# Down projections: the gate and the addition of x1 spread one step per entry, and x1 for the norm loaded one tile per entry

## The chip, the cores and the metric

The kernel runs as one program on one core of a Trainium2 chip. The metric is the device time of one execution in microseconds (us). The kernel before took 2372.89 us, the median of three runs from 2371.21 to 2376.52. The profile shows one further execution of it.

## The reference, cut to what matters

One decoder layer over 2048 rows of width 1024. Attention and short convolution come first, then the ConvFFN, in whose last lines everything around this change lies:

```python
    x = x + g1 * (mixed @ w_out)                          # called x1 below

    h2 = rmsnorm(x, norm2_g) * (1 + sc2) + sh2
    u = causal_dwconv(h2 @ w_up, ffn_conv_w)
    u_gate, u_val = jnp.split(u, 2, axis=-1)
    y = (jax.nn.silu(u_gate) * u_val) @ w_down            # D_FF = 2816 to 1024
    return x + g2 * y
```

All tensors are float32. What is computed at the end is therefore, for each block of the output, a sum of matrix products, times the gate g2, plus x1.

## The kernel before, in words

**Stages.** The rows are worked in two halves of 1024 rows. The stages follow each other on TensorE: mixing (attention, convolution, output projection), then up(0), down(0), up(1), down(1), where up computes `h2 @ w_up` with convolution and silu for one half, and down the product with `w_down`. The norm of the second half (row blocks Q = 2 and 3 of 512 rows each) is not done ahead: its work, `norm2_late(2)` and `norm2_late(3)`, runs inside down(0) as side work. x1 lies in DRAM by then (`x1_sc`, one tensor for each 128 rows).

**A down projection.** It is one level of Strassen-Winograd multiplication: seven products p = 0 to 6 (the table `plan`) yield four output blocks of 512 rows by 512 columns. Each product sums over j = 0 to 10 (D_FF / 256 = 11 steps). `todo` lists the 77 pairs (p, j), here called entries. Four PSUM tiles `acc[t]`, t = 0 to 3, hold 128 rows each of the sum. An entry's operands come as one raw tile of two halves (y and w, 256 KB each), which ScalarE and VectorE split into a high part `hi` (L1528) and a low part `lo` = raw - hi (L1529). Each acc tile of an entry then takes three matmuls, hi by hi, hi by lo, lo by hi, so an entry is 12 matmuls of 128x128 by 128x512 (L1762). The entry j = 9 issues none, and j = 10 does those of 9 and 10 together, tile by tile, so that tile t is complete 6 matmuls after tile t - 1.

**Order within an entry.** `K` keeps instructions in the order in which the program issues them, on each engine. An entry issues in this order: the split (hi, lo) of the operands of the entry two ahead, the loads of raw tiles five ahead (SyncE's queue, SP; four raw buffers), stores that were put off (`flush`), the loads of x1 for an output block (`x1_tiles`, at the entries that `extra` names), the matmuls, at j = 10 the evictions `evict(p, t)`, and one step of the side work (`next(side)`). VectorE and ScalarE therefore see evictions and side work in one line with the splits that the coming entries need.

**Evictions.** Products 0 to 2 and 3 to 6 build sums in `u2` and `u3`. A block is finished in product 1 (block (0, 0): row half 0, column half 0), 4 (block (0, 1)), 5 (block (1, 1)) and 6 (block (1, 0)). Finishing is `finish_block`: multiply by the gate (L1715), add x1 (`xs`, through `add`, L1440), store to `out` (L1717). In products 4, 5 and 6 an addition with u2 or u3 stands ahead of it. All of it is issued for a tile at once, at that tile's eviction. Products 0, 2, 3 and 5 begin in fresh PSUM tiles (`banks`); products 1, 4 and 6 add on to the tiles of the product before them, so that the first matmul of product 6 on tile t waits for product 5's eviction of that tile.

**Side work in down(0).** A step of `norm2_late` is taken per entry. In order: the last three steps of up's last pair (they store y and its differences), then for Q = 2 the loads of x1 (L1353, four transfers of 512 KB in one step), three empty steps, four steps with one squaring each on ScalarE (L1358), the row factors, the scaling (L1365), and then transposes, `hi`/`lo` pairs and sums (L1260, L1267, L1408). For Q = 3 the same follows, with more sums per step on VectorE.

Of the kernel before, what the change touches and what calls it, by code (L numbers as in the profile page):

```python
# [9 lines left out]
F32 = mybir.dt.float32  # L10
F32R = mybir.dt.float32r
F16 = mybir.dt.float16
BF16 = mybir.dt.bfloat16
I32 = mybir.dt.int32
AF = mybir.ActivationFunctionType
# [5 lines left out]
P = 128  # L21
S = 2048
D = 1024
# [19 lines left out]
NTEMP = 7  # L43
# [3 lines left out]
def kernel(  # L47
# [19 lines left out]
    nc = tc.nc  # L67
    V, A, G, T = nc.vector, nc.scalar, nc.gpsimd, nc.tensor
    x, c, out = x[0], c[0:1], out[0]
# [71 lines left out]
    K = tc.keep_in_program_order  # L141
# [1101 lines left out]
    with ExitStack() as ph:  # L1243
# [25 lines left out]
        xn = {}  # L1269
# [78 lines left out]
        def norm2_late(Q):  # L1348

            ss = fp.tile([P, 16], F32, tag="ss", name="ss", bufs=2)[:, 0:4]  # L1350
            xn[Q] = [wide_temp()[:, 0:D] for _ in range(4)]
            for t in range(4):
                K(nc.sync.dma_start(xn[Q][t], x1_sc[Q * 4 + t]))  # L1353
            for _ in range(3):
                yield
            for t in range(4):
                junk = fp.tile([P, D], BF16, tag="t2", name="junk", bufs=NTEMP)
                K(A.activation(junk, xn[Q][t], AF.Square, accum_out=ss[:, t : t + 1]))  # L1358
                yield
            K(V.tensor_scalar(ss, ss, 1.0 / D, EPS, op0=ALU.mult, op1=ALU.add))  # L1360
            for ins in rsqrt_steps(fp, ss, 4, "r"):
                K(ins)
            yield
            for t in range(4):
                K(V.tensor_scalar(xn[Q][t], xn[Q][t], ss[:, t : t + 1], None, op0=ALU.mult))  # L1365
                if t % 2:
                    yield
            later = []
            if Q % 2 == 0:
                for k in range(4):  # L1370
                    for n, name in enumerate(("b11", "b21")):
                        affine = turn(Q, 4 * n + k)
                        if later:
                            later.pop()()
                        yield
                        h = affine()
                        hi, lo = pair(name, k)
                        high(h, hi)
                        later.append(lambda h=h, hi=hi, lo=lo: low(h, hi, lo))
                        yield  # L1380
                later.pop()()
                yield
                return

            def sums(k, b1, b2):

                b22, t1s, t2s, t3s, t4s = [pair(name, k) for name in ("b22", "t1", "t2", "t3", "t4")]
                b11, b21 = bt["b11", k], bt["b21", k]
                t3 = temp()
                high(b2, b22[0])  # L1390
                diff(t3, b2, b1)
                diff(b1, b1, b11[0])
                diff(b1, b1, b11[1])
                low(b2, *b22)
                yield
                high(b1, t1s[0])
                high(t3, t3s[0])
                yield
                diff(b2, b2, b1)
                low(b1, *t1s)  # L1400
                low(t3, *t3s)
                yield
                high(b2, t2s[0])
                yield
                t4 = temp()
                diff(t4, b21[1], b2)
                low(b2, *t2s)
                K(V.tensor_tensor(t4, t4, b21[0], op=ALU.add))  # L1408
                yield
                high(t4, t4s[0])  # L1410
                yield
                low(t4, *t4s)
                yield

            running = []

            def go_on():
                for g in list(running):
                    if next(g, 1):
                        running.remove(g)  # L1420

            for k in range(4):
                first = turn(Q, k)
                go_on()
                yield
                b1 = first()
                go_on()
                yield
                second = turn(Q, 4 + k)
                go_on()  # L1430
                yield
                b2 = second()
                go_on()
                running.append(sums(k, b1, b2))
                yield
            while running:
                go_on()
                yield
# [251 lines left out]
        def down(hv, side):  # L1690

            todo = [(p, j) for p in range(7) for j in range(NJ)]
            loaded = split = 3
            rows = [[slice((Q * 4 + t) * P, (Q * 4 + t + 1) * P) for t in range(4)] for Q in (2 * hv, 2 * hv + 1)]
            u2, u3 = [[fb.tile([P, 512], F32, tag=f"src{4 * n + t}", name="u") for t in range(4)] for n in range(2)]
            gate = [gates[:, D + n * 512 : D + (n + 1) * 512] for n in range(2)]
            xs = {}

            def x1_tiles(c, n):
                xs[c, n] = [fb.tile([P, 512], F32, tag=f"wo{4 * c + t}1", name="xs") for t in range(4)]  # L1700
                for xp, r in zip(xs[c, n], rows[c]):
                    K(nc.sync.dma_start(xp, x1_sc[r.start // P][:, n * 512 : (n + 1) * 512]))

            def banks(kinds):
                return [
                    ps_d.tile([P, 512], F32, tag="d", name="acc") if k == "d" else ps_u.tile([P, 512], F32, tag="u", name="acc")
                    for k in kinds
                ]

            def rest():  # L1710
                return fp.tile([P, 1024], F32, tag="first", name="g", bufs=2)[:, 0:512]

            def finish_block(c, n, t, total):
                g = rest()
                K(V.tensor_tensor(g, total, gate[n], op=ALU.mult))  # L1715
                add(xs[c, n][t], xs[c, n][t], g)
                K(nc.sync.dma_start(out[rows[c][t], n * 512 : (n + 1) * 512], xs[c, n][t]))  # L1717

            def evict(p, t):
                a = acc[t]  # L1720
                if p == 0:
                    K(A.activation(u2[t], a, AF.Copy))
                elif p == 1:
                    finish_block(0, 0, t, a)
                elif p == 2:
                    add(u2[t], u2[t], a)
                elif p == 3:
                    add(u3[t], u2[t], a)
                elif p == 5:
                    add(u3[t], u3[t], a)  # L1730
                    finish_block(1, 1, t, u3[t])
                else:
                    g = rest()
                    add(g, u2[t], a)
                    finish_block(*((0, 1) if p == 4 else (1, 0)), t, g)

            extra = {(1, 2): (0, 0), (4, 2): (0, 1), (5, 2): (1, 1), (6, 3): (1, 0)}
            for e, (p, j) in enumerate(todo):
                while split < min(e + 3, len(todo)):
                    if loaded == split:  # L1740
                        raws[todo[loaded]] = load_operands(hv, *todo[loaded])
                        loaded += 1
                    pairs[todo[split]] = split_pair(raws.pop(todo[split]))
                    split += 1
                while loaded < min(e + 6, len(todo)):
                    raws[todo[loaded]] = load_operands(hv, *todo[loaded])
                    loaded += 1
                if (p, j) in ((0, 0), (0, 4)):
                    flush()
                if (p, j) in extra:  # L1750
                    x1_tiles(*extra[p, j])
                if j == 0 and p in (0, 2, 3, 5):
                    acc = banks({0: "dddd", 2: "uuud", 3: "dddu", 5: "uudd"}[p])
                if j != NJ - 2:
                    for t in range(4):
                        c = slice(t * P, (t + 1) * P)
                        for jj in (j,) if j < NJ - 1 else (j - 1, j):
                            yh, yl, wh, wl = pairs[p, jj]
                            for a, b, st, sp in (
                                (yh, wh, jj == 0 and p in (0, 2, 3, 5), False), (yh, wl, False, False), (yl, wh, False, jj == NJ - 1)  # L1760
                            ):
                                K(T.matmul(acc[t], lhsT=a[:, c], rhs=b, start=st, stop=sp, skip_group_check=True))  # L1762
                        if j == NJ - 1:
                            evict(p, t)
                next(side, None)
            for _ in side:
                pass
# [39 lines left out]
```

## Time and profile before

| | |
|---|---|
| median of three runs | 2372.89 us (2371.21 to 2376.52) |
| the profiled execution | 2373.66 us, span 2372.0 us, mean granted TensorE clock 0.994 |
| busy share of the span | PE 96%, VectorE (DVE) 73%, ScalarE (ACT) 49%, GpSimd (POOL) 14% |
| down(0), 1518.5 to 1752.8 us | PE busy 223.63 of 234.30 us, DVE 167.62 us |
| up(1), 1752.8 to 2151.3 us | PE busy 398.50 of 398.50 us |
| down(1), 2151.3 to 2364.5 us | PE busy 211.14 of 213.20 us, DVE 127.77 us |
| after the last matmul, 2364.5 to 2372.0 us | 7.50 us, PE idle |

The span runs from the first to the last instruction; the device time has 1.66 us around it. Times inside the span are given from its start. A row of the timeline holds the start, the duration, the engine, the line and the operation, output <- inputs, and in brackets how long the engine sat idle before it and what released it. PE is TensorE's matmul stream, and a wait of PE lengthens the kernel wherever nothing later absorbs it.

### The profile page before, as it was taken

How to read it: one execution, taken by the hardware profiler on the slowest of the kernel's cores; microseconds unless marked ns; L12 is line 12 of the kernel's file. 1: busy time of each engine (PE TensorE's matmuls, PEld its weight loads, DVE VectorE, ACT ScalarE, POOL GpSimd, SP SyncE). 2: the span in 40 equal slices, each digit the busy share in tenths (PEclk: the TensorE clock that was granted, in tenths of full speed). 3: DMA queues.
4: the chain of work that ended last, by engine and by line, in shares of the span. 5: the costliest groups of instructions: out<-in, count | busy, mean ns of one | idle time of the engine just before them, and what ended most of it. 6: DMA issues, size and time to landing. Idle time of an engine off the chain costs nothing.

```text
span 2372.0 us, 38568 instructions
## 1 busy us (share of the span) xinstructions
PE 2276.3 (96%) x14208; PEld 1358.2 (57%) x14208; DVE 1740.4 (73%) x3404; ACT 1163.1 (49%) x1990; POOL 339.3 (14%) x282
## 2 busy tenths in 40 slices
PE   5899999999899898999999999999999999999998
PEld 5764554444677676444444444578764444447886
DVE  6768886673999897456999999866955566566556
ACT  5745453321788887343556555455522222224333
POOL 0211111111677884001000000000000000000000
PEclk9999999999999999999999999999999999999999
DMA  9346589963799997434465556676654454545765
GB/s 280 139 153 179 162 261 292 305 219 89 156 176 193 209 189 156 159 111 169 172 215 196 208 209 217 232 234 221 221 197 156 149 162 133 164 164 195 226 199 209
DMA packets 452646, 455.25 MB, mean 192 GB/s; under 512 B 191248, under 2 KB 301160, under 8 KB 451432
## 3 DMA queue, kind: packets, MB, share of 16 engines
q1 hardware_dynamic: 445336, 435.94, 62.0%
q10 hardware_dynamic: 4752, 8.46, 1.0%
q0 software_dynamic: 2368, 8.39, 0.9%
q8 instruction: 111, 1.82, 0.3%
q14 instruction: 79, 0.65, 0.1%
HBM read 284.84 MB, written 134.28 MB: 177 GB/s over the span
## 4 chain that ended last, share of the span: by engine, by line
PE 78%; DVE 11%; DMA 4%; ACT 4%; issue 2%; SPq 1%; POOL 0%; DVEq 0%; ACTq 0%; POOLq 0%
PE acc L1605 28%; PE acc L1762 15%; PE acc L145 13%; PE pr L145 11%; PE pv L145 2%; DMA far<-wide 2%; PE pt L1107 2%; DVE s_t L1070 1%; PE ps L1046 1%; DVE near L1114 1%; PE ps L1047 1%; PE po L1143 1%; DVE t L1440 1%; ACT s_t L1087 1%; PE po L1145 1%
## 5 line engine op out<-in xcount | busy, mean ns | idle before, releaser
L1605 PEld LDWEIGHTS <-pair 128*128 128x128 f16 x3696 | 361.5, 98 | 439.7 <-issue 5.0
L1605 PE MATMUL acc<-t,pair 128*128 128x512 f16 x2112 | 477.3, 379 | 1.9 <-DVE t L1440 1.9
L1605 PE MATMUL acc<-b,pair 128*128 128x512 f16 x1584 | 363.4, 379 | 0.0
L1529 DVE TENSOR_TENSOR lo<-raw,hi 128x1024 fp32r<-128x1024 f32 x154 | 186.8, 1223 | 135.0 <-ACT hi L1528 126.0
L1618 DVE SCALAR_TENSOR_TENSOR w<-w,fcw,w 128x1024 f32<-128x1024 f32 x176 | 226.1, 1285 | 79.4 <-ACT w L1613 73.2
L1528 ACT ACTIVATE hi<-raw 128x1024 fp32r<-128x1024 f32 x154 | 161.0, 1056 | 184.6 <-PE acc L1762 110.2
L1762 PE MATMUL acc<-hi 128*128 128x512 f32 x616 | 243.9, 396 | 5.5 <-DVE u L1440 2.8
L1762 PE MATMUL acc<-lo,hi 128*128 128x512 f32 x616 | 242.1, 393 | 7.2 <-DVE lo L1529 7.2
L1762 PE MATMUL acc<-hi,lo 128*128 128x512 f32 x616 | 241.6, 392 | 0.0
L145 PEld LDWEIGHTS <-h 128*128 128x128 f16 x1344 | 130.3, 98 | 97.5 <-DVE h L358 5.4
L1613 ACT ACTIVATE w<-w,fcw 128x1024 f32<-128x1024 f32 x88 | 100.7, 1144 | 160.7 <-DVE w L1440 160.7
L145 PE MATMUL acc<-wp,mp 128*128 128x512 f16 x768 | 171.1, 382 | 1.1 <-DVE raw L999 1.0
L1087 ACT ACTIVATE s_t<-s_t,nb,cst 128x2048 f32<-128x2048 f32 (+15 forms) x128 | 164.7, 1288 | 4.8
L1099 POOL TENSOR_TENSOR wide<-s_t,wide 128x1024 f16<-128x1024 f32 x64 | 136.8, 2138 | 5.3
L1762 PEld LDWEIGHTS acc<-lo,hi 128*128 128x128 f32 x616 | 116.8, 190 | 33.0 <-DVE lo L1529 9.3
L1762 PEld LDWEIGHTS acc<-hi 128*128 128x128 f32 x616 | 116.5, 189 | 31.9 <-DVE u L1440 4.5
L1070 DVE CUSTOM_DVE_ANT_0 s_t<-ps,nf,mx 128x512 f32<-128x512 f32 (+1 forms) x192 | 119.5, 643 | 16.9 <-PE ps L1049 8.6
L1762 PEld LDWEIGHTS acc<-hi,lo 128*128 128x128 f32 x616 | 116.6, 189 | 24.7
L145 PE MATMUL pr<-h,wh 128*128 128x512 f16 x576 | 126.5, 379 | 0.0
L145 PEld LDWEIGHTS <-mp 128*128 128x128 f16 x768 | 75.3, 98 | 88.9 <-issue 3.6
L145 PE MATMUL pr<-h,wl 128*128 128x512 f16 x576 | 125.8, 379 | 0.0
L1046 PE MATMUL ps<-kh,qs 128*128 128x512 f16 (+1 forms) x320 | 109.9, 347 | 12.5 <-DVE mx L1070 10.9
(362 smaller groups left out, 4084.8 us busy)
## 6 DMA issues: line engine op xcount, KB each, us to landing
up_sc<-pair SPq DMA_DIRECT2D x132, 256.0 KB, 2.7
pair<-up_sc SPq DMA_DIRECT2D x132, 256.0 KB, 3.0
wx<-in_w_up_dram SPq DMA_DIRECT2D x88, 256.0 KB, 3.7
raw<-in_w_up_dram SPq DMA_DIRECT2D x44, 512.0 KB, 3.8
y_t<-t SPq DMA_DIRECT2D x88, 256.0 KB, 2.6
raw<-y_t SPq DMA_DIRECT2D x88, 256.0 KB, 4.0
raw<-w_sc SPq DMA_DIRECT2D x88, 256.0 KB, 4.6
y_b<-y SPq DMA_DIRECT2D x66, 256.0 KB, 2.0
```

What stands on the lines that cost most here:

```text
L145: ins = T.matmul(acc, lhsT=a, rhs=b, start=st, stop=sp)
L1046: K(T.matmul(ps[:, 0:cw], lhsT=qt, rhs=kh[:, c0 : c0 + cw], start=True, stop=False))
L1070: K(V.tensor_tensor_reduce(out=s_t[:, o0 + c0 : o0 + c0 + cw], in0=ps[:, 0:cw], in1=nf[:, c0 : c0 + cw], scale=1.0, scalar=-3.0e38 if g == ...
L1087: K(A.activation(cols, cols, AF.Exp, bias=nb[:, p : p + 1], scale=qk[:, 4:5], accum_out=un["l"][:, p : p + 1]))
L1099: K(G.tensor_tensor(wide[:, 1, :], s_t[:, WB * P : WU], wide[:, 0, :], op=ALU.subtract))
L1107: K(T.transpose(pt[:, b * P : (b + 1) * P], s_t[:, (b0 + b) * P : (b0 + b + 1) * P], ident))
L1528: K(A.activation(hi, raw, AF.Copy))
L1529: K(V.tensor_tensor(lo, raw, hi.bitcast(F32), op=ALU.subtract))
L1605: K(T.matmul(acc, lhsT=a, rhs=b, start=st, stop=sp, skip_group_check=True))
L1613: K(A.activation(y, u[:, 0:1024], AF.Copy, scale=fcw[:, ct : ct + 1]))
L1618: K(V.scalar_tensor_tensor(y, u[:, m : m + 1024], fcw[:, m * 44 + ct : m * 44 + ct + 1], y, op0=ALU.mult, op1=ALU.add))
L1762: K(T.matmul(acc[t], lhsT=a[:, c], rhs=b, start=st, stop=sp, skip_group_check=True))
```

## The change

What it does, by part:

- `norm2_late` issues its four loads of x1 in four steps, one each, and squares each tile three steps after its load. The steps with squarings are the same steps as before.
- An eviction only takes the sum out of PSUM: for products 1 and 6 multiplied by the gate, for 4 added to u2, for 5 added to u3. What is left (gate, addition of x1, store) goes into a list, `later`, of which each entry of the products 0 to 5 issues one step, and each of product 6 two, after its split and loads and ahead of its matmuls.
- The last block, (1, 0), is gate * (u2 + acc) + x1. gate * u2 and its addition to x1 are now steps of product 6, ahead of the end; at the end acc is multiplied by the gate and added. That takes two more VectorE instructions per tile over the product, and one less at the end.
- The buffers of x1 tiles are named otherwise (block (1, 0) takes those of column half 0's first row blocks, `wo0` to `wo3`), and (1, 0)'s x1 is loaded at entry (6, 1), before (6, 3). The tile `g` is used in two halves.

```diff
-            for t in range(4):
-                K(nc.sync.dma_start(xn[Q][t], x1_sc[Q * 4 + t]))
-            for _ in range(3):
-                yield
-            for t in range(4):
-                junk = fp.tile([P, D], BF16, tag="t2", name="junk", bufs=NTEMP)
-                K(A.activation(junk, xn[Q][t], AF.Square, accum_out=ss[:, t : t + 1]))
+            for t in range(7):
+                if t < 4:
+                    K(nc.sync.dma_start(xn[Q][t], x1_sc[Q * 4 + t]))
+                if t >= 3:
+                    junk = fp.tile([P, D], BF16, tag="t2", name="junk", bufs=NTEMP)
+                    K(A.activation(junk, xn[Q][t - 3], AF.Square, accum_out=ss[:, t - 3 : t - 2]))
                 yield
...
-                xs[c, n] = [fb.tile([P, 512], F32, tag=f"wo{4 * c + t}1", name="xs") for t in range(4)]
+                xs[c, n] = [fb.tile([P, 512], F32, tag=f"wo{4 * (c and n) + t}1", name="xs") for t in range(4)]
...
+            later, spare = [], []
+
             def rest():
-                return fp.tile([P, 1024], F32, tag="first", name="g", bufs=2)[:, 0:512]
-
-            def finish_block(c, n, t, total):
-                g = rest()
+                if not spare:
+                    g = fp.tile([P, 1024], F32, tag="first", name="g", bufs=2)
+                    spare.extend((g[:, 0:512], g[:, 512:1024]))
+                return spare.pop(0)
+
+            def gated(g, total, n):
                 K(V.tensor_tensor(g, total, gate[n], op=ALU.mult))
+
+            def put_out(c, n, t, g):
                 add(xs[c, n][t], xs[c, n][t], g)
                 K(nc.sync.dma_start(out[rows[c][t], n * 512 : (n + 1) * 512], xs[c, n][t]))
...
-                elif p == 1:
-                    finish_block(0, 0, t, a)
+                elif p in (1, 6):
+                    g = rest()
+                    gated(g, a, 0)
+                    later.append(lambda: put_out(p == 6, 0, t, g))
...
+                elif p == 4:
+                    g = rest()
+                    add(g, u2[t], a)
+                    later.append(lambda: gated(g, g, 1))
+                    later.append(lambda: put_out(0, 1, t, g))
                 elif p == 5:
                     add(u3[t], u3[t], a)
-                    finish_block(1, 1, t, u3[t])
-                else:
-                    g = rest()
-                    add(g, u2[t], a)
-                    finish_block(*((0, 1) if p == 4 else (1, 0)), t, g)
-
-            extra = {(1, 2): (0, 0), (4, 2): (0, 1), (5, 2): (1, 1), (6, 3): (1, 0)}
+                    later.append(lambda: gated(u3[t], u3[t], 1))
+                    later.append(lambda: put_out(1, 1, t, u3[t]))
+                    later.append(lambda: gated(u2[t], u2[t], 0))
+
+            def with_x1(t):
+                later.append(lambda: add(xs[1, 0][t], xs[1, 0][t], u2[t]))
+
+            extra = {(1, 2): (0, 0), (4, 2): (0, 1), (5, 2): (1, 1), (6, 1): (1, 0)}
...
+                if (p, j) == (6, 5):
+                    for t in range(4):
+                        with_x1(t)
+                for _ in range(1 if p < 6 else 2):
+                    if later:
+                        later.pop(0)()
...
                             evict(p, t)
+                            while later and p == 6:
+                                later.pop(0)()
```

**Where the order changes.** Three places are shown. The first is SyncE's queue in product 0 of down(0), where the x1 of Q = 2 is loaded; `w` is a tile for x1 (512 KB), `raw` an operand tile, `y_t` a store of up's last pair. Before:

```order
L1353 DMA w_18823<-x_sc_87 128x1024
L1353 DMA w_18824<-x_sc_88 128x1024
L1353 DMA w_18825<-x_sc_89 128x1024
L1353 DMA w_18826<-x_sc_90 128x1024
L1539 DMA raw<-y_b_9_104 128x512
L1546 DMA raw<-in_w_down_dram 128x512
L1565 DMA y_t_10_149<-t_18625 128x512
L1565 DMA y_t_10_160<-t_18797 128x512
L1565 DMA y_t_10_171<-t_18797 128x512
L1539 DMA raw<-y_b_10_105 128x512
L1546 DMA raw<-in_w_down_dram 128x512
```

The same place after the change:

```order
L1354 DMA w_18823<-x_sc_87 128x1024
L1538 DMA raw<-y_b_9_104 128x512
L1545 DMA raw<-in_w_down_dram 128x512
L1564 DMA y_t_10_149<-t_18625 128x512
L1564 DMA y_t_10_160<-t_18797 128x512
L1564 DMA y_t_10_171<-t_18797 128x512
L1354 DMA w_18824<-x_sc_88 128x1024
L1538 DMA raw<-y_b_10_105 128x512
L1545 DMA raw<-in_w_down_dram 128x512
L1354 DMA w_18825<-x_sc_89 128x1024
L1538 DMA raw<-y_b_0_106 128x512
L1545 DMA raw<-in_w_down_dram 128x512
```

Three of the four x1 transfers moved behind the operands of j = 9, and two behind those of j = 10.

The second is VectorE at the end of product 4 in down(0); `g<-u,acc` is the eviction, `t` and `b` are side work for Q = 3, `lo` a split. Before, the last two of four tiles and what follows:

```order
L1440 TENSOR_TENSOR g<-u,acc 128x512
L1715 TENSOR_TENSOR g<-g,gates 128x512
L1440 TENSOR_TENSOR xs<-xs,g 128x512
L1440 TENSOR_TENSOR g<-u,acc 128x512
L1715 TENSOR_TENSOR g<-g,gates 128x512
L1440 TENSOR_TENSOR xs<-xs,g 128x512
L1260 TENSOR_TENSOR t_19944<-t_20049,t_19944 128x512
L1267 TENSOR_TENSOR t_20022<-t_20022,t_19970 128x512
L1260 TENSOR_TENSOR t_20054<-t_19970,t_20054 128x512
L1260 TENSOR_TENSOR t_20056<-t_20058,t_20056 128x512
L1529 TENSOR_TENSOR lo<-raw,hi 128x1024 x2
L1267 TENSOR_TENSOR t_20185<-b_19350,t_20022 128x512
```

After, from the eviction of the first tile:

```order
L1439 TENSOR_TENSOR g<-u,acc 128x512 x4
L1260 TENSOR_TENSOR t_19942<-t_20047,t_19942 128x512
L1267 TENSOR_TENSOR t_20020<-t_20020,t_19968 128x512
L1260 TENSOR_TENSOR t_20052<-t_19968,t_20052 128x512
L1260 TENSOR_TENSOR t_20054<-t_20056,t_20054 128x512
L1528 TENSOR_TENSOR lo<-raw,hi 128x1024
L1718 TENSOR_TENSOR g<-g,gates 128x512
L1528 TENSOR_TENSOR lo<-raw,hi 128x1024
L1439 TENSOR_TENSOR xs<-xs,g 128x512
L1267 TENSOR_TENSOR t_20168<-b_19346,t_20020 128x512
```

Eight of the twelve instructions of the evictions moved behind the next splits, where one stands behind each `lo`.

The third is the end of VectorE's program, in product 6 of down(1). Before, the evictions of the four tiles, which end the program:

```order
L1440 TENSOR_TENSOR g<-u,acc 128x512
L1715 TENSOR_TENSOR g<-g,gates 128x512
L1440 TENSOR_TENSOR xs<-xs,g 128x512
L1440 TENSOR_TENSOR g<-u,acc 128x512
L1715 TENSOR_TENSOR g<-g,gates 128x512
L1440 TENSOR_TENSOR xs<-xs,g 128x512
L1440 TENSOR_TENSOR g<-u,acc 128x512
L1715 TENSOR_TENSOR g<-g,gates 128x512
L1440 TENSOR_TENSOR xs<-xs,g 128x512
L1440 TENSOR_TENSOR g<-u,acc 128x512
L1715 TENSOR_TENSOR g<-g,gates 128x512
L1440 TENSOR_TENSOR xs<-xs,g 128x512
```

After, the last two splits and what follows them; `xs<-xs,u` adds gate * u2 to x1:

```order
L1439 TENSOR_TENSOR xs<-xs,u 128x512 x2
L1528 TENSOR_TENSOR lo<-raw,hi 128x1024
L1439 TENSOR_TENSOR xs<-xs,u 128x512 x2
L1528 TENSOR_TENSOR lo<-raw,hi 128x1024
L1718 TENSOR_TENSOR g<-acc,gates 128x512
L1439 TENSOR_TENSOR xs<-xs,g 128x512
L1718 TENSOR_TENSOR g<-acc,gates 128x512
L1439 TENSOR_TENSOR xs<-xs,g 128x512
L1718 TENSOR_TENSOR g<-acc,gates 128x512
L1439 TENSOR_TENSOR xs<-xs,g 128x512
L1718 TENSOR_TENSOR g<-acc,gates 128x512
L1439 TENSOR_TENSOR xs<-xs,g 128x512
```

Two instructions per tile are left behind the last matmuls in place of three. Neither TensorE's, ScalarE's nor GpSimd's order changes.

## The prediction

> **What bounds the kernel now.** I read the busy time by stage first, then TensorE's waits in the two down projections, then the timeline around each wait. The windows give, behind each stretch, its length and the busy time of PE, PEld, DVE, ACT and POOL, then the granted clock, the DMA share and GB/s:
>
> ```profile
> 1518.50:1752.80 234.30, 223.63 (x991) 182.16 (x990) 167.62 (x215) 116.26 (x141) 0.00 (x0) 0.98 0.70 229
> 2151.30:2364.50 213.20, 211.14 (x926) 173.02 (x924) 127.77 (x129) 81.69 (x80) 0.00 (x0) 1.00 0.65 217
> 2364.50:2372.00 7.50, 0.00 (x0) 0.00 (x0) 4.09 (x7) 0.00 (x0) 0.00 (x0) 0.74 0.27 105
> ```
>
> PE sets the time of both down projections; it idles 10.7 us in down(0), 2.1 in down(1), and 7.5 us pass after the last matmul. Who made it wait (us in total, times, longest), first in down(0), then in down(1):
>
> ```profile
> PE acc L1762 <- DVE lo L1529: 6.6, 3, 5.1
> PE acc L1762 <- ACT hi L1528: 2.7, 2, 1.5
> PE acc L1762 <- DVE u L1440: 1.4, 2, 1.1
> ```
>
> ```profile
> PE acc L1762 <- DVE u L1440: 1.4, 2, 1.1
> PE acc L1762 <- DVE lo L1529: 0.6, 1, 0.6
> ```
>
> The timeline puts the longest of them in four places:
>
> ```profile
> 1544.88 0.49 PE L1762 MATMUL acc<-hi 128*128 128x512 f32 x1 [1.46 <-ACT hi L1528]
> 1693.91 0.79 PE L1762 MATMUL acc<-lo,hi 128*128 128x512 f32 x1 [5.06 <-DVE lo L1529]
> 1724.59 0.50 PE L1762 MATMUL acc<-hi 128*128 128x512 f32 x1 [1.09 <-DVE u L1440]
> 2308.00 0.50 PE L1762 MATMUL acc<-lo,hi 128*128 128x512 f32 x1 [0.64 <-DVE lo L1529]
> ```
>
> I call them A (1544, end of product 0 of down(0); with its neighbours 6.6 - 5.1 + 2.7 = 4.2 us), B (1694, start of product 5, 5.1 us), C (1724, from product 5 to 6, 1.4 us) and D (down(1), 1.4 + 0.6 = 2.0 us). The granted clock behind A, B and C, in the sixth column after the stretch:
>
> ```profile
> 1549.40:1552.10 2.70, 2.70 (x7) 2.13 (x7) 1.26 (x2) 2.70 (x5) 0.00 (x0) 0.50 0.68 223
> 1693.90:1698.80 4.90, 4.89 (x12) 3.82 (x13) 4.83 (x8) 1.32 (x2) 0.00 (x0) 0.50 0.74 219
> 1724.60:1729.00 4.40, 4.40 (x19) 3.65 (x20) 4.37 (x5) 1.06 (x1) 0.00 (x0) 1.00 0.71 232
> ```
>
> After A, PE runs 2.70 us at half clock, after B 4.90 us, which costs half of each: 1.35 and 2.45 us. C leaves the clock alone. So A is worth 5.55 us, B 7.5, C 1.4, D 2.0.
>
> **The x1 loads (A).** What SP issues and what ACT then waits for:
>
> ```profile
> 1530.73 1.90 SPq L1353 DMA_DIRECT2D w<-x_sc  x4
> 1533.35 0.90 SPq L1546 DMA_DIRECT2D raw<-in_w_down_dram  x1
> 1540.08 0.33 SPq L1546 DMA_DIRECT2D raw<-in_w_down_dram  x1
> 1543.78 1.06 ACT L1528 ACTIVATE hi<-raw 128x1024 fp32r<-128x1024 f32 x1 [5.46 <-DMA raw<-in_w_down_dram]
> 1547.00 1.06 ACT L1528 ACTIVATE hi<-raw 128x1024 fp32r<-128x1024 f32 x1 [1.13 <-DMA raw<-in_w_down_dram]
> ```
>
> ```profile
> 1529.20:1547.00 17.80, 15.45 (x66) 11.93 (x64) 7.66 (x8) 7.27 (x9) 0.00 (x0) 1.00 0.97 324
> ```
>
> The DMA engines are full (0.97) at 324 GB/s. The operands of j = 9 and 10 queue behind 2 MB of x1 and land at about 1543.7 and 1546.9; PE ran dry at 1544.88 - 1.46 = 1543.4. By the order shown, three of the four x1 tiles go behind j = 9 and two behind j = 10. Up to j = 10 there then stand y's stores (512 KB), j = 8, one x1, j = 9, `y_t` (768), a second x1 and j = 10, 512 each where not said: 3840 KB or 3.93 MB, at 324 GB/s 12.1 us from 1529.2, so 1541.3. With hi (1.06) and lo (1.23) it is ready at 1543.7; PE needs its lo after three matmuls of j = 9 and one more, at 1543.4 + 4 x 0.23 = 1544.3. No wait if transfers end in turn; if j = 10 shares the engines with the 1 MB issued behind it (the third x1, j = 11), it lands 3.2 us later and PE waits 2.6 us. I take 0.8, as the queue holds them in this order and the first end is nearer. A saves 4.75 us. The squarings keep their steps, each three steps (8 us) behind its load.
>
> **The evictions in down(0) (B and C).** PE's pace and start of product 5, then VectorE's line around B:
>
> ```profile
> 1653.43 5.50 PE acc L1762 x24
> ```
>
> ```profile
> 1682.89 0.48 PE L1762 MATMUL acc<-hi 128*128 128x512 f32 x1
> 1688.46 0.39 PE L1762 MATMUL acc<-hi 128*128 128x512 f32 x1
> ```
>
> ```profile
> 1682.03 0.68 DVE L1440 TENSOR_TENSOR g<-u,acc 128x512 f32<-128x512 f32 x1
> 1682.74 0.69 DVE L1715 TENSOR_TENSOR g<-g,gates 128x512 f32<-128x512 f32 x1
> 1683.47 0.69 DVE L1440 TENSOR_TENSOR xs<-xs,g 128x512 f32<-128x512 f32 x1
> 1684.08 0.68 DVE L1440 TENSOR_TENSOR g<-u,acc 128x512 f32<-128x512 f32 x1
> ...
> 1690.23 0.68 DVE L1260 TENSOR_TENSOR t<-t,t 128x512 f16<-128x512 f32 x1
> 1690.83 0.69 DVE L1267 TENSOR_TENSOR t<-t,t 128x512 f32<-128x512 f32 x1
> 1691.43 1.29 DVE L1260 TENSOR_TENSOR t<-t,t 128x512 f16<-128x512 f32 x2
> 1692.63 2.35 DVE L1529 TENSOR_TENSOR lo<-raw,hi 128x1024 fp32r<-128x1024 f32 x2
> 1694.91 0.69 DVE L1267 TENSOR_TENSOR t<-b,t 128x512 f32<-128x512 f16 x1
> ...
> 1699.37 1.22 DVE L1529 TENSOR_TENSOR lo<-raw,hi 128x1024 fp32r<-128x1024 f32 x1
> ```
>
> 24 matmuls take 5.50 us: 0.229 each, 2.75 per entry. Product 5 starts at 1682.89, and two entries later, at 1688.46, PE stands: the lo of entry (5, 2) comes out of the pair begun at 1692.63, behind twelve eviction instructions (8.2 us) and four of side work. An instruction that uses its forerunner's result starts 0.72 us after it, another 0.61.
>
> After the change four evictions at 0.61 end at 1684.47, the side work (2.40) at 1686.87, lo (5, 2) at 1688.1: before PE wants it, at 1688.69. B's wait goes. What is late next is found by counting on: one postponed step (0.61), lo (5, 3) (1.14), another step (0.61), then seven side instructions (1694.91 to 1699.37, 4.46 us) and lo (5, 4), which ends at 1696.05; PE wants it at 1688.69 + 5.50 = 1694.2. So 1.9 us of waiting comes back at (5, 4). Counting further to (5, 6) and (5, 10), with fewer side instructions each time, gives 0.3 and 0.4 more: 2.6 us left. B saves 7.5 - 2.6 = 4.9 us.
>
> The Trainium skill ("TensorE: Matmul & The Clock Gate", section "Why this matters for your kernels") asks for no idle gaps over some 3 us, lest the clock fall to half. B's row agrees, with 4.90 us at 0.50 behind a gap of 5.06; A's doesn't quite: no single gap there exceeds 1.46 us, and the clock halved. By that rule the 1.9 us left at B brings no slow clock with it, and the sum is as I make it.
>
> By A's row alone the clock could fall there for another 1.35 us of cost; I leave it out of the sum and within the range.
>
> C: the four u3 additions now follow each other at 0.61 in place of 2.05 us, PE delivers a tile each 6 x 0.229 = 1.37 us, and product 6 no longer waits for them: 1.4 saved. In product 6 an entry costs VectorE 1.14 + 0.61 + 0.72 = 2.5 of 2.75 us, so the eight instructions added per half lie beside PE; the additions of x1 come five entries behind their loads. The loads for product 6 stand behind fewer stores at a time.
>
> **Down(1) (D) and the end.** There is no side work there; without two thirds of each eviction the splits are ahead of PE, and D's 2.0 us go. The end:
>
> ```profile
> 2364.09 0.39 PE L1762 MATMUL acc<-hi,lo 128*128 128x512 f32 x1
> ```
>
> ```profile
> 2360.44 0.69 DVE L1440 TENSOR_TENSOR g<-u,acc 128x512 f32<-128x512 f32 x1 [4.48 <-PE acc L1762]
> 2368.04 0.69 DVE L1440 TENSOR_TENSOR xs<-xs,g 128x512 f32<-128x512 f32 x1
> ```
>
> Before, tile 0 starts at 2360.44 and 12 instructions, 2.05 us a tile, are through at 2368.73. Now a tile takes 1.33, less than PE's 1.37; the last starts at 2364.55 and ends at 2365.95. 2.8 us saved, at least the 2.05 of one tile's time, and the last store follows as before.
>
> **Sum.** 4.75 + 4.9 + 1.4 + 2.0 + 2.8 = 15.85. From the profiled execution's 2373.66 us that leaves 2357.8; the median of the runs shown lies 0.77 below it, so 2357.0. All losses gone would be 5.55 + 7.5 + 1.4 + 2.0 + 2.8 = 19.3, that is 2353.6.
>
> **Rivals.** First, VectorE stays the bound in product 5: its side work and postponed steps add up, ScalarE's hi waits with them, and B's 7.5 us come back but for 0 to 2. For it: no row quoted from 1682.03 on has an idle time in brackets. Against: the count above. 2357.0 + 4.9 = 2361.9; chance 0.18.
>
> Second, A stays, since all bytes still pass in the same 20 us: 2.6 us of waiting and 1.35 of clock, 3.2 more than I count: 2360.2; chance 0.12.
>
> Third, the gain is absorbed in down(0): VectorE's total sets its length, and only D and the end (4.8 us) remain: 2368.1, within 0.2%, or 4.7 us, about what a measurement of this kernel can tell from no change. Chance 0.06.
>
> Fourth, slower: SP's queue. A store now waits for an addition that stands behind the lo of the entry two ahead, and the next raw load stands behind that store. With four raw buffers the round is step or steps (0.6 to 1.4), issue (0.8), landing, hi (1.06) and lo (1.23) in four entries, 11.0 us.
>
> ```profile
> raw<-w_sc SPq DMA_DIRECT2D x22, 256.0 KB, 4.8
> ```
>
> At 4.8 us a round takes 8.5 to 9.3 us, and no wait arises. It decides from a landing of 6.5 to 7.3 us; at 9 us each round loses about 2.2 us, and 36 entries carry steps, 9 rounds, 20 us: 2377. Chance 0.06.
>
> The Trainium skill ("VectorE: DVE Perf Modes", "Rules for kernel authors") says to lessen the count of chained instructions, not their semaphores. By it the 16 added would cost 16 x 0.69 = 11 us of VectorE and spacing them win nothing; the row's 0.72 against 0.61 contradicts the second half, and product 6's slack covers the first.
>
> **Chances and range.** Forecast 0.58 (2353.6 to 2359.5). Faster by over 0.2%: 0.58 + 0.18 + 0.12 = 0.88; same 0.06; slower 0.06. The range runs from 2353.0, all losses gone with little over, to 2366.0, the first two rivals together (2357.0 + 4.9 + 3.2 = 2365.1) with a little for the spread of runs.
>
> **What would show it.** Right: no wait of PE around the end of product 0, one of about 2 us at entry (5, 4) of down(0) in place of 5.1 at (5, 2), none by `u`, none in down(1), and 4.7 us from the last matmul to the end. Wrong: half clock in product 5, ACT waiting for raw tiles in product 0, or SP waiting for `xs` ahead of raw loads that PE then misses.

## The result and the profile after

The changed kernel takes 2357.93 us, the median of six runs (2355.91 to 2360.74); beside it the kernel before took 2373.92 (six runs). The ratio is 0.9933, with a 95% interval from 0.9921 to 0.9944: faster by 0.7%. Predicted were 2357.0 us within 2353.0 to 2366.0. Here and in the table below, medians and ratios are without two slow runs, one of 3966.71 us (norm loads only) and one of 4803.49 us (the changed kernel once more).

The profiled execution took 2358.7 us, span 2357.0 us. First the windows of it: down(0), up(1), down(1), and the stretch behind the last matmul:

```profile
1520.40:1743.90 223.50, 219.50 (x991) 179.38 (x990) 170.16 (x223) 116.47 (x141) 0.00 (x0) 1.00 0.73 241
1743.90:2142.50 398.60, 398.60 (x1849) 180.68 (x1849) 234.78 (x262) 113.20 (x177) 0.00 (x0) 1.00 0.48 155
2142.50:2352.30 209.80, 209.80 (x926) 173.42 (x924) 131.05 (x137) 81.80 (x80) 0.00 (x0) 1.00 0.67 221
2352.30:2357.00 4.70, 0.03 (x1) 0.00 (x0) 1.45 (x3) 0.00 (x0) 0.00 (x0) 0.96 0.36 137
```

Against the stretches of before, down(0) went from 234.3 to 223.5 us, up(1) stayed (398.5 and 398.6), down(1) went from 213.2 to 209.8 with no wait of PE left, and the end from 7.5 to 4.7. Only 1.9 us go the other way: down(0) starts at 1520.4, not 1518.5, though nothing ahead of it was changed. Over the profiles of this study it starts between 1517.7 and 1523.3, so this is scatter, and from here on a kernel's down projections are compared from their own first matmul to their last. Counted so, down(0) takes 233.84 us before and 223.18 after, down(1) 212.79 and 209.42.

Who made PE wait in down(0) now:

```profile
PE acc L1781 <- DVE lo L1528: 3.0, 4, 1.7
PE acc L1781 <- ACT hi L1527: 0.9, 1, 0.9
```

10.7 us became 3.9, and `u` is gone from the list. The same waits in the timeline:

```profile
1546.83 0.50 PE L1781 MATMUL acc<-hi 128*128 128x512 f32 x1 [0.85 <-ACT hi L1527]
1548.09 0.50 PE L1781 MATMUL acc<-lo,hi 128*128 128x512 f32 x1 [0.76 <-DVE lo L1528]
1693.40 0.50 PE L1781 MATMUL acc<-lo,hi 128*128 128x512 f32 x1 [1.74 <-DVE lo L1528]
1708.64 0.50 PE L1781 MATMUL acc<-lo,hi 128*128 128x512 f32 x1 [0.21 <-DVE lo L1528]
1739.17 0.50 PE L1781 MATMUL acc<-lo,hi 128*128 128x512 f32 x1 [0.30 <-DVE lo L1528]
```

The first two are what is left of A, at the operands of j = 10. The third is entry (5, 4), the wait that the prediction had counted out there as 1.9 us; the fourth is (5, 10). The fifth, in the last entry of product 6, was not foreseen. The clock stays at 1.00 throughout down(0). VectorE behind the evictions of product 4, and the end of its program:

```profile
1679.39 2.47 DVE L1439 TENSOR_TENSOR g<-u,acc 128x512 f32<-128x512 f32 x4
1684.19 1.22 DVE L1528 TENSOR_TENSOR lo<-raw,hi 128x1024 fp32r<-128x1024 f32 x1
1692.12 1.22 DVE L1528 TENSOR_TENSOR lo<-raw,hi 128x1024 fp32r<-128x1024 f32 x1
...
2348.29 0.69 DVE L1718 TENSOR_TENSOR g<-acc,gates 128x512 f32<-128x512 f32 x1 [2.30 <-PE acc L1781]
2353.09 0.69 DVE L1439 TENSOR_TENSOR xs<-xs,g 128x512 f32<-128x512 f32 x1
```

Four evictions take 2.47 us in a row, lo (5, 2) starts 4.8 us after the first of them (before: 10.6), and lo (5, 4) 12.7 us after. The last addition ends at 2353.78, 1.45 us behind the last matmul's end (2352.33).

### The profile page after: what moved, and what is told of

The parts are those of the page before. It is cut to its first block, busy times and chain, and to the rows that moved or that the text cites. A ratio compares the mean times of both kernels' runs of the same rounds, so it can differ in the third digit from the quotient of the medians.

```text
span 2357.0 us, 38562 instructions
## 1 busy us (share of the span) xinstructions
PE 2273.1 (96%) x14208; PEld 1357.6 (58%) x14208; DVE 1740.0 (74%) x3412; ACT 1163.1 (49%) x1990; POOL 339.3 (14%) x282
## 4 chain that ended last, share of the span: by engine, by line
PE 79%; DVE 11%; ACT 4%; DMA 3%; issue 2%; SPq 1%; POOL 0%; DVEq 0%; ACTq 0%
PE acc L1604 28%; PE acc L1781 15%; PE acc L145 13%; PE pr L145 11%; PE pv L145 2%; DVE s_t L1070 2%; PE pt L1107 2%; PE ps L1046 1%; DVE near L1114 1%; PE ps L1047 1%; DMA far<-wide 1%; ACT s_t L1087 1%; PE po L1143 1%; DVE t L1439 1%; PE po L1145 1%
```

## The experiments

Each kernel was timed beside the kernel before on the same chip, in five rounds. Not all rows come from one chip, so rows are compared by their ratios rather than by their medians, except for the last two, which ran side by side. The column of down(0) is from its first matmul's start to its last's, in the one profiled execution.

| kernel | median, us | ratio to before, 95% interval | down(0), us |
|---|---|---|---|
| before | | 1 | 233.84 |
| changed | 2357.93 | 0.9933 (0.9921 to 0.9944) | 223.18 |
| norm loads only | 2370.95 | 0.9981 (0.9969 to 0.9994) | 229.53 |
| evictions only | 2360.68 | 0.9939 (0.9924 to 0.9955) | 228.18 |
| last block not ahead | 2360.14 | 0.9938 (0.9921 to 0.9954) | 223.39 |
| steps held to (5, 6) | 2358.21 | 0.9929 (0.9914 to 0.9945) | 223.42 |
| norm two entries later | 2359.59 | 0.9941 (0.9929 to 0.9952) | 225.50 |
| steps held, spread | 2358.41 | 0.9934 (0.9921 to 0.9948) | 221.18 |
| burst three entries later | 2365.04 | 0.9963 (0.9952 to 0.9975) | 229.01 |
| a gap between the loads | 2360.19 | 0.9944 (0.9932 to 0.9956) | 223.44 |
| gap and held steps | 2354.18 | 0.9917 (0.9904 to 0.9931) | 220.27 |
| changed, once more | 2358.03 | 0.9933 (0.9920 to 0.9946) | 222.25 |

The changed kernel's two profiles differ by 0.9 us in down(0), so a difference of that size in one profile shows nothing by itself.

**Norm loads only.** The edit is the first hunk of the change, put into the kernel before:

```diff
...
+            for t in range(7):
+                if t < 4:
+                    K(nc.sync.dma_start(xn[Q][t], x1_sc[Q * 4 + t]))
...
```

> The kernel before with the x1 loads for the norm spread one per entry, and nothing else of the change. Theory (each loss stands by itself): the waits at the end of product 0 of down(0) and the half clock behind them shrink from 6.6 us, counted from matmul start to matmul start, to about 2.1, as in the changed kernel; B (5.1 us of waiting at entry (5, 2)), C, D and the 7.5 us behind the last matmul stay as before. Time 4.5 us under the kernel before. Rival (VectorE's total work sets the length of down(0)): PE arrives earlier at product 5, the wait at B grows from 5.1 to about 9.5 us, and the time is that of the kernel before.

The waits in its down(0), and the longest of them:

```profile
PE acc L1761 <- DVE lo L1528: 5.8, 2, 5.1
PE acc L1761 <- DVE u L1439: 1.4, 2, 1.1
PE acc L1761 <- ACT hi L1527: 1.0, 1, 1.0
```

```profile
1691.63 0.80 PE L1761 MATMUL acc<-lo,hi 128*128 128x512 f32 x1 [5.05 <-DVE lo L1528]
```

B is as long as before (5.05 and 5.06) and C is unchanged; what is left of A is 1.8 us of waiting, 2.2 from start to start. Down(0) is 4.3 us shorter, and the ratio says the same (0.19%, 4.5 us, with an interval from 1.4 to 7.4). The theory holds: VectorE's line follows PE's pace, so this wait, taken away in product 0, isn't paid back in product 5.

**Evictions only.** The other way round: the changed kernel with the first hunk undone.

```diff
-            for t in range(7):
-                if t < 4:
...
+            for t in range(4):
+                K(nc.sync.dma_start(xn[Q][t], x1_sc[Q * 4 + t]))
+            for _ in range(3):
+                yield
...
```

> The changed kernel with the four x1 loads for the norm in one step again, so only the evictions are changed. Theory: A stays (waits of 4.2 us and half clock for 2.7 us at the end of product 0), B falls to 2 to 2.9 us, C and D go, 4.7 us are left behind the last matmul: 4.5 us over the changed kernel, 11 to 12.5 under the one before. Rival (the parts need each other, as transfers late in product 0 push VectorE's work back): B keeps over 4 us of waiting, and the time lies 7 us or more over the changed kernel.

Its waits in down(0), then a window of the clock behind the first of them:

```profile
PE acc L1782 <- DVE lo L1529: 3.3, 4, 1.7
PE acc L1782 <- ACT hi L1528: 2.4, 1, 2.4
```

```profile
1547.80:1554.00 6.20, 6.17 (x15) 4.88 (x16) 4.36 (x15) 3.76 (x6) 0.00 (x0) 0.50 0.68 219
```

A is back, with 3.75 us of waiting and 6.2 us at half clock, and product 5 waits as in the changed kernel (1.7 at (5, 4)). Down(0) is 5.0 us longer than there, down(1) and the end are alike (209.42, 4.7). The gains of the two parts add, as far as one profile of each can tell: 4.3 us of the loads and 5.7 of the evictions in down(0), 10.0 together, against 10.7 for both.

**Last block not ahead.**

```diff
...
+                elif p == 6:
+                    g = rest()
+                    add(g, u2[t], a)
+                    later.append(lambda: gated(g, g, 0))
+                    later.append(lambda: put_out(1, 0, t, g))
...
-                    later.append(lambda: gated(u2[t], u2[t], 0))
...
-                if (p, j) == (6, 5):
-                    for t in range(4):
-                        with_x1(t)
```

> The changed kernel with the last block finished as before: u2 added at the eviction of product 6, then gate, x1 and store, three instructions per tile behind the matmuls, nothing of it ahead. Theory: a tile takes 2.05 us again where PE delivers one each 1.37, the four tiles queue up, and 7.5 in place of 4.7 us pass behind the last matmul: 2.8 us over the changed kernel; in down(0) nothing changes, as up(1) does not wait. Rival (only the last tile's own chain counts): one instruction more, 0.7 us.

The last tile's three instructions, in a span of 2362.8 us:

```profile
2357.50 0.68 DVE L1439 TENSOR_TENSOR g<-u,acc 128x512 f32<-128x512 f32 x1
2358.21 0.69 DVE L1718 TENSOR_TENSOR g<-g,gates 128x512 f32<-128x512 f32 x1
2358.94 0.69 DVE L1439 TENSOR_TENSOR xs<-xs,g 128x512 f32<-128x512 f32 x1
```

The last matmul ends at 2355.4, and 7.5 us follow, against 4.7: 2.8 us, the queue of four tiles, not one tile's 0.7. Down(0) stays at 223.4. The ratios, 0.9938 and 0.9933, lie within each other's intervals; the profile decides.

**Steps held to (5, 6), then two per entry.**

```diff
-                for _ in range(1 if p < 6 else 2):
+                for _ in range(1 if p < 5 else 2 if p > 5 or j > 5 else 0):
```

> The changed kernel with the postponed steps of product 4 held back until entry (5, 6), then two per entry, so that they stand behind most of the norm's side work. Theory (the wait left at entry (5, 4) is made by the two steps, 1.2 us, and the four evictions, 2.4 us, in VectorE's line): the wait there falls from 1.7 to about 0.5 us, and the time by 1.3 to 1.6 us. Rival (the seven side instructions alone make it, or ScalarE's hi behind them): the wait stays at 1.5 us or more and so does the time.

PE's waits at (5, 4) and at the first entry of product 6:

```profile
1692.18 0.50 PE L1781 MATMUL acc<-lo,hi 128*128 128x512 f32 x1 [0.53 <-DVE lo L1528]
1712.60 0.47 PE L1781 MATMUL acc<-hi 128*128 128x512 f32 x1 [0.76 <-DVE u L1439]
```

The wait at (5, 4) falls to 0.53, as the theory has it. The time doesn't fall: product 5 is 0.7 us shorter (32.35 us) and product 6 0.7 longer. The held steps crowd the end of product 5, the evictions of u3 come late, and a new wait of 0.76 us stands at product 6; the one in its last entry is 0.60, against 0.30. The expectation was right on the wait and wrong on the time.

**Steps held and spread.** Held until (5, 5), one per entry from there, the last two in (6, 0).

```diff
-            extra = {(1, 2): (0, 0), (4, 2): (0, 1), (5, 2): (1, 1), (6, 1): (1, 0)}
+            extra = {(1, 2): (0, 0), (4, 2): (0, 1), (5, 2): (1, 1), (6, 2): (1, 0)}
...
-                for _ in range(1 if p < 6 else 2):
+                for _ in range(2 if p > 5 else 1 if p < 5 or j > 4 else 0):
```

> The changed kernel with the postponed steps of product 4 held until entry (5, 5), then one per entry, the last two in (6, 0), and x1 of block (1, 0) loaded at (6, 2). Theory (VectorE has 31.5 us of work for the 30.3 us of product 5, and only steps that leave the product shorten it): 0.5 us at (5, 4) and none at the first entry of product 6, 1 to 1.5 us under the changed kernel. Rival (held steps always come back as waits for u at product 6, as in the run with two per entry): 0.7 us or more there, no gain.

```profile
PE acc L1781 <- DVE lo L1528: 1.3, 2, 0.8
PE acc L1781 <- ACT hi L1527: 1.1, 1, 1.1
PE acc L1781 <- DVE u L1439: 0.2, 1, 0.2
```

0.8 and 1.1 of it are A. Product 5 is left with 0.5, product 6 with 0.2. Down(0) is 221.18 us, 1.1 to 2.0 under the two profiles of the changed kernel; the medians cannot tell them apart.

**Norm two entries later.**

```diff
-        down(0, chain(up(0), steps[2], steps[3], kept_first()))
+        down(0, chain(up(0), (None for _ in range(2)), steps[2], steps[3], kept_first()))
```

> The changed kernel with the norm's side work in down(0) begun two entries later, so that all x1 loads for Q = 2 come behind the operands of j = 10. Theory (A's rest, 2.0 us, is bytes ahead of j = 10: 1 MB less at about 270 GB/s lands 3.9 us earlier): no wait of PE at the end of product 0; at product 5 the side work stands two entries later, seven instructions now right behind the four evictions, and 1 to 2 us more of waiting comes up there. Time 0 to 1 us under the changed kernel. Rival (A's rest comes from SP, whose loads wait for raw buffers and earlier transfers): the wait at the end of product 0 stays at 1.5 us or more.

Its only kind of wait, and the two longest:

```profile
PE acc L1781 <- DVE lo L1528: 5.6, 5, 2.2
```

```profile
1697.36 0.50 PE L1781 MATMUL acc<-lo,hi 128*128 128x512 f32 x1 [2.18 <-DVE lo L1528]
1708.52 0.50 PE L1781 MATMUL acc<-lo,hi 128*128 128x512 f32 x1 [1.57 <-DVE lo L1528]
```

A is gone entirely, so the x1 loads ahead of j = 10 made it, and SP's waits for buffers, the rival, did not; their bytes and the time to issue them were not told apart. But products 5 and 6 now wait for 5.6 us, and down(0) is 2.3 us longer than in the changed kernel, where the time was expected to fall by 0 to 1 us: product 5 now holds 60 VectorE instructions in place of 53, and they cost more than counted.

**Burst three entries later.** The four loads in one step, as before, but behind three empty steps; evictions as changed.

```diff
...
-        down(0, chain(up(0), steps[2], steps[3], kept_first()))
+        down(0, chain(up(0), (None for _ in range(3)), steps[2], steps[3], kept_first()))
```

> The changed evictions with the four x1 loads in one step again, but the norm's side work begun three entries later. Theory (A is bytes ahead of the operands of j = 9 and 10, of which PE needs both within one entry): behind those the same 2 MB cost little, at most 1 us of waiting around the end of product 0 and the start of product 1, against 4.4 us and half clock with the loads three entries earlier. Rival (2 MB at once always stall: only the spreading helps): 3 us or more of waiting at the first two entries of product 1.

The wait at the first entry of product 1, then two in product 6 and the clock behind them:

```profile
1551.63 0.50 PE L1782 MATMUL acc<-hi 128*128 128x512 f32 x1 [1.55 <-ACT u L1728]
1735.36 0.51 PE L1782 MATMUL acc<-hi 128*128 128x512 f32 x1 [1.20 <-ACT hi L1528]
1736.62 0.50 PE L1782 MATMUL acc<-lo,hi 128*128 128x512 f32 x1 [0.75 <-DVE lo L1529]
```

```profile
1736.60:1741.00 4.40, 4.38 (x12) 3.49 (x13) 4.40 (x6) 3.17 (x3) 0.00 (x0) 0.61 0.60 231
```

1.55 us lies between the theory's 1 and the rival's 3. The place of the 2 MB matters more than their coming at once, but the burst isn't free. ScalarE's copies of product 0's sums (`u`) stand in line behind a split that waits 3.94 us for its raw tile:

```profile
1550.03 1.06 ACT L1528 ACTIVATE hi<-raw 128x1024 fp32r<-128x1024 f32 x1 [3.94 <-DMA raw<-in_w_down_dram]
1550.99 2.04 ACT L1728 ACTIVATE u<-acc 128x512 f32<-128x512 f32 x4
```

By the order of SP's queue, that tile's loads (1542.00 and 1542.49) are the first behind the four x1 loads (1538.72 on); this link is read from the order, not tried. The rest of its 229.0 us lies in products 5 and 6, which take 36.4 and 34.0 us, against 33.1 and 30.3 in the changed kernel. Product 5 holds 63 VectorE instructions, the price of the later side work, as in the run with the norm two entries later. What made ScalarE late in product 6 stays open.

**A gap between the loads.** One step without a load behind the first tile, all else one entry later.

```diff
...
+            at = (0, 2, 3, 4) if Q == 2 else (0, 1, 2, 3)
+            for s in range(at[3] + 4):
...
```

> The changed kernel with a step without a load between the first and the second x1 tile of Q = 2, so that one tile less stands ahead of j = 10 and all later side work moves by one entry. Theory: the wait at the end of product 0 falls from 2.0 to about 0.7 us (0.5 MB less ahead, 1.9 us); in product 5 the seven side instructions now come one entry later than the evictions' neighbours, lo (5, 4) is in time, and 0.5 to 1 us is left at (5, 5). Time about 2 to 2.5 us under the changed kernel. Rival (VectorE's total in product 5 decides, not where the side work lies): the waits in product 5 sum to 2.5 us as now, only A's 1.3 us are gained.

```profile
PE acc L1783 <- DVE lo L1530: 3.4, 4, 1.8
```

No wait of note is left at the end of product 0. In product 5 the wait only moved, to entry (5, 5), where it is 1.83 us, and down(0) takes 223.4 us as in the changed kernel. The theory of this run falls. The rival holds for product 5: VectorE's total decides there, not which entry the seven instructions stand in. But the gain of 1.3 us that it expected at A doesn't show: later side work brought 57 VectorE instructions into product 5 in place of 53, and products 5 and 6 together take 1.8 us longer.

**Gap and held steps.** The gap between the loads together with the steps held and spread.

> Both of the last edits: a step without a load behind the first x1 tile, and the postponed steps of product 4 held until (5, 5), x1 of block (1, 0) loaded at (6, 2). Theory (VectorE's total in product 5 decides what is left): no wait at the end of product 0, under 1 us in product 5, at most 1 us in product 6; from the first to the last matmul of down(0) about 220.5 us, against 223.2 in the changed kernel and 221.2 with the held steps alone. Rival (side work moved by an entry costs in products 5 and 6 what it gains in product 0): 221 us or more.

The waits in down(0), and its window:

```profile
PE acc L1783 <- DVE lo L1530: 0.6, 2, 0.4
PE acc L1783 <- ACT hi L1529: 0.5, 1, 0.5
```

```profile
1518.50:1739.20 220.70, 219.55 (x991) 179.45 (x990) 170.03 (x223) 116.44 (x141) 0.00 (x0) 1.00 0.73 244
```

1.15 us of waiting is left of 10.7, and down(0) takes 220.27 us, as expected. This version took 2354.18 us. Against the steps held and spread alone (221.18) that is 0.9 us less, no more than two profiles of one kernel differ by, so what the gap adds is not shown.

**The changed kernel once more**, on the same chip:

> The changed kernel itself beside it, on the same chip, for the comparison: waits in down(0) as in its first profile (2.0 us at the end of product 0, 2.6 in product 5), 223 us from the first to the last matmul of down(0). By the theory 2.5 us over the other kernel of this call, by the rival within 1.5.

```profile
PE acc L1781 <- DVE lo L1528: 2.7, 3, 1.8
PE acc L1781 <- ACT hi L1527: 0.2, 1, 0.2
```

2358.03 us, with 2.9 us of waits: A's rest is 0.96 us here and was 1.61 in the first profile, product 5 is alike, and the wait in product 6 is missing. The better version is 3.9 us ahead by the medians and 2.0 by down(0); the ratios 0.9917 and 0.9933 overlap in their intervals, so the profile shows the direction and the size stays loose.

## Why the prediction was right

To compare terms, a wait is counted from one matmul's start to the next, less the usual 0.228 us; this takes in the half clock.

| term | predicted, us | measured, us |
|---|---|---|
| A, x1 loads | 4.75 | 6.64 - 2.09 = 4.55 |
| B, product 5 | 4.9 | 7.80 - 2.85 = 4.95 |
| C, product 5 to 6 | 1.4 | 1.94 - 0 = 1.94 |
| product 6 | 0 | -0.6 |
| D, down(1) | 2.0 | 212.79 - 209.42 = 3.37 |
| the end | 2.8 | 7.47 - 4.67 = 2.80 |
| sum | 15.85 | 17.01 |

The medians moved by 15.99 us. The profiled spans moved by 15.0: down(0) started 1.87 us later, and its rows in the table add up to 10.84, 0.2 more than it became shorter (10.66). That 15.99 lies so close to 15.85 is in part luck. The terms came out 1.2 us larger, and the starts of down(0) alone scatter by more than that.

*What bounds the kernel.* Right. The losses lay in the four places named, and at the end; the runs with the loads alone, the evictions alone and the last block not ahead each brought back the losses of the part left out and no others.

*A.* The mechanism was right: fewer bytes ahead of j = 10, a shorter wait. That the saving came out near, 4.55 for 4.75, is luck: two errors, of 1.3 and 1.1 us, nearly cancelled. The first is what is left. Traffic did not end in turn: j = 10's last transfer was issued at 1538.13 and hi started at 1545.72 (below), 14.6 us after the second of y's stores was issued (1531.08), where the prediction, counting from the same store, had 12.1 for the end without sharing. At 340 GB/s, the rate of that stretch, 14.6 us are 5.0 MB, so about 1 MB of what was issued behind it shared the engines. The wait, 1.6 us in brackets and 2.09 from start to start, lies beyond the 0.8 I took, nearer to the other end (2.6). So the sign "no wait of PE around the end of product 0" failed, and ScalarE did wait for a raw tile there. The second error is the loss before the change, counted from idle times in brackets and the half clock as 5.55 us, where starts give 6.64. The half clock that I left out of the sum did not come.

```profile
1538.13 0.45 SPq L1545 DMA_DIRECT2D raw<-in_w_down_dram  x1
1545.72 1.06 ACT L1527 ACTIVATE hi<-raw 128x1024 fp32r<-128x1024 f32 x1 [1.59 <-DMA raw<-in_w_down_dram]
```

```profile
1531.00:1546.00 15.00, 14.98 (x67) 12.06 (x65) 7.65 (x8) 7.66 (x10) 0.00 (x0) 1.00 0.99 340
```

*B.* Right step by step: 1.9 us counted for (5, 4), 1.74 measured; 0.4 for (5, 10), 0.21 measured; nothing at (5, 6) but a gap of 0.29 between starts. The first rival, VectorE still the bound with B back in full, did not come. Its reason is real, though: what is left of B is VectorE's total, as the held steps show (221.18) and as the later side work shows (225.50). Product 5 in the changed kernel, with the steps held and spread, and with the norm two entries later; VectorE's busy time is the third after the length:

```profile
1680.25:1713.32 33.07, 30.98 (x136) 24.63 (x134) 32.42 (x44) 15.38 (x20) 0.00 (x0) 1.00 0.76 228
1680.33:1711.64 31.31, 30.53 (x136) 24.63 (x134) 30.25 (x41) 15.80 (x20) 0.00 (x0) 1.00 0.70 223
1677.35:1713.20 35.85, 31.81 (x140) 24.95 (x139) 35.20 (x49) 17.57 (x24) 0.00 (x0) 1.00 0.69 217
```

VectorE is busy all but 0.6 to 1.1 us of product 5 each time, and the product's length follows its work.

*C and D.* The mechanism was right, the sizes too small. The step at fault is the reading of a wait as the idle time in brackets. A wait of 0.64 us at 2308.00 stood for a gap of 1.03 between starts, 0.80 over the usual, and the next start came 0.1 late as well. For D these gaps sum to 2.8; the other 0.5 of the 3.37 is not in the run with the loads alone, whose down(1) is that of the kernel before and takes 212.33 us, so it is scatter. The 16 added instructions of the prediction are 8 by net count, as the end loses one per tile; no term hangs on it.

*Product 6.* "No wait" was wrong by little: 0.3 us in its last entry in one of two profiles of the changed kernel. In other versions it was up to 0.6 there, and up to 1.2 in earlier entries (the later burst), behind its first entry always for operands that come late. It was not settled whether the x1 loads at (6, 1) make it: the wait in the last entry is missing with them at (6, 2), but steps were held back there too, and it is missing or under 0.15 us as well in three profiles with them at (6, 1) (the changed kernel once more, the last block not ahead, the evictions alone).

*The end.* Right, and shown by the run without the part added ahead: a queue of four tiles at 2.05 us each against PE's 1.37.

*The other rivals.* A did not stay: the run with the loads alone has 1.8 us of it, and no half clock behind. Nothing was absorbed: the run with the loads alone shortened down(0) by A alone. SP's stores cost PE nothing in products 2 to 4; the waits of product 5 were for `lo`, with VectorE's line full; and in product 6 they cost no more than the 0.3 us above.

## What to carry to other kernels

Work that an engine does at the end of a block delays the operand of the entry behind it, so count that engine's line on to the next three or four needs: the first comes free and the next one is late by what the count says. Moving work within a stretch where the engine's total is the limit only moves the wait (223.42 us with the steps held to (5, 6), 223.18 without); it shrinks when work leaves the stretch (221.18), and grows when an edit elsewhere pushes work into it (225.50). So an edit that takes away an earlier wait by delaying other work can gain nothing (the gap, 223.44). Whether it gains once there is room for what it delays lies within the scatter here (220.27 with the gap and the steps held and spread, 221.18 without the gap).

## What the runs showed of the hardware

Whether a wait brings the half clock is not told by its length. One wait of 2.18 us left the clock at 1.00 (the run with the norm two entries later); waits of 1.20 and 0.75 us, 2 us in all, brought 0.61 over the 4.4 us behind them (the later burst); 0.85 and 0.76 in the changed kernel did not. In all twelve profiles the granted clock changes only at the ends of stretches of 3.41 us that follow each other without a break, and half clock lasts one or two of them wherever matmuls go on behind it. What counts is how long PE is idle within one such stretch. These are stretches of the kernel before (A), then of the norm two entries later, then three of the later burst:

```profile
1545.42:1548.83 3.41, 1.24 (x3) 0.48 (x3) 1.41 (x2) 2.28 (x4) 0.00 (x0) 1.00 0.91 283
1548.83:1552.25 3.42, 2.88 (x7) 2.31 (x8) 1.90 (x3) 3.42 (x7) 0.00 (x0) 0.50 0.68 229
1693.53:1696.95 3.42, 1.65 (x8) 1.03 (x6) 3.35 (x5) 1.99 (x4) 0.00 (x0) 1.00 0.95 362
1700.05:1703.46 3.41, 1.61 (x7) 1.35 (x8) 3.41 (x6) 3.06 (x4) 0.00 (x0) 1.00 0.29 112
1734.19:1737.60 3.41, 1.49 (x5) 1.04 (x6) 2.26 (x3) 2.05 (x2) 0.00 (x0) 1.00 1.01 364
1737.60:1741.01 3.41, 3.41 (x9) 2.64 (x9) 3.41 (x5) 2.18 (x3) 0.00 (x0) 0.50 0.47 180
```

The first has 2.2 us of idle PE and half clock follows; the third and fourth have 1.8 and full clock goes on; the fifth has 1.9 and half clock follows. From the start of down(0) to the last matmul this holds in all twelve profiles: no stretch with up to 1.8 us of idle is followed by half clock, and each with 1.9 or more is. In the stages ahead of it the two sides overlap between 1.65 and 1.96 us, so the bound is not sharp. Once the clock is halved, a stretch with 0.64 us of idle kept it so (the evictions alone), and one with 0.54 ended it (A).

The Trainium skill ("TensorE: Matmul & The Clock Gate", section "What's actually happening") states a window of about 3.4 us that runs freely; these rows agree, with 3.41. Its advice to avoid idle gaps over some 3 us (section "Why this matters for your kernels") is not enough here, as 1.9 us of idle within one stretch sufficed.

A bracket's idle time is less than what the wait costs PE: 5.06 us in the bracket were 5.22 over the usual distance of starts, 0.76 were 1.03, and 0.64 were 0.80.
